# Two of four weight-block sums as transfers that add in SBUF, in a two-layer hybrid attention trunk

## The chip, the cores and the metric

The kernel runs on one core of one Trainium2 chip. The metric is the device time of one execution in microseconds (us); the median of several runs of each kernel counts. All arithmetic is in fp32. TensorE multiplies, VectorE (DVE), ScalarE (ACT) and GpSimd (POOL) do the elementwise work, SyncE (SP) issues most transfers, and each engine works through its own instructions strictly in order. Issuing engines other than SP put their transfers into that same order: a transfer that GpSimd issues waits its turn among GpSimd's instructions.

## The reference

A sequence of 512 tokens with 1024 features passes through two layers. Each has a feed-forward stage, a token mixer (latent attention in layer 0, a compressed, selected and windowed attention in layer 1), and a second feed-forward stage:

```python
def swiglu(x, w_gate, w_up, w_down):
    return (jax.nn.silu(x @ w_gate) * (x @ w_up)) @ w_down

for i in range(DEPTH):                       # DEPTH = 2
    h = h + 0.5 * swiglu(rmsnorm(h, ffn_norm_a[i]), ffn_a_w_gate[i], ffn_a_w_up[i], ffn_a_w_down[i])
    m = rmsnorm(h, mix_norm[i])
    h = h + mixer(m)
    h = h + 0.5 * swiglu(rmsnorm(h, ffn_norm_b[i]), ffn_b_w_gate[i], ffn_b_w_up[i], ffn_b_w_down[i])
return rmsnorm(h, final_norm)
```

Gate and up matrices are 1024 x 2816, the down matrix 2816 x 1024. There are four feed-forward stages; the change touches these alone.

## The kernel before, in words

**Precision.** Every fp32 operand of a product is split in two tiles, high and low: ACT rounds it to the high tile (L170, or L143 for weights of a plain slab), DVE subtracts to get the low tile (L171, L145). A product is three matmuls, high by high, high by low and low by high.

**A feed-forward stage** (`ffn`) runs over 22 blocks of 128 hidden units. Blocks 0 to 2 are multiplied plainly (`plain`). While they run, the inputs are combined for the other blocks (`combine`, tiles `u` and `four`), the row of norms comes out (`row`), and ACT and DVE do the gates (`gate`, tile `tg`: silu at L376) and their products (`act`, tiles `tu`, `ah`, `al`). Blocks 3 to 21, that is 19 in each stage and 76 in all, use a scheme of seven products in place of eight on half blocks: `wsums` prepares the weight blocks and `product` multiplies one of them.

**The weight sums of one block** (`wsums`, L306 to L343). SP loads the gate slab `rg` (L315; the tile is called `rg` in the first block of a stage, `wr` in the others) and the up slab `ru` (L317), each 128 x 1024. Their halves of 512 columns are g0, g1, u0 and u1. In order, the code:

- splits g0 and g1 as loaded (weights 1 and 2),
- puts s1 = u0 + u1 into the tile `s1` (L336, shown as `s` in the profile),
- adds g0 to u0 in place (L337) and splits `ru`, which now holds u0 + g0 and u1 (weights 7 and 4),
- adds s1 to g0 in place (L339), then that sum to g1 in place (L340), and splits both (weights 6 and 3),
- splits s1 (weight 5).

So there are four DVE sums of 128 x 512 a block. Raw `wr` tiles have two buffers; the tag "fr", which `ru`, the first block's `rg` and, in the first stage, the tiles `xt` of the input share, has three; `s1` has one.

**The seven products** go in the order 1, 7, 6, 2, 5, 4, 3. Between them ACT copies partial results out of PSUM (L481, L483, L485, L488: tiles `pg`, `uq`), since the later products add to them. After a block's products come its gate, and two or three `unit`s of the down-projection of blocks that are done: each loads a slab `wdr` of 128 x 384 from SP (L405, two buffers), splits it into `wd` (L170, L171), multiplies it and adds the result to `h` (L399).

**What sets the order.** The code is written in its natural order, and a scheduler places each engine's instructions ahead of time: it may take the split of a later block ahead of the evictions of the present one, and issue a load as early as buffers allow. What it has placed is run in order, each instruction waiting for its semaphores. GpSimd issues nothing in the feed-forward stages of this kernel; at their ends and in the mixers it does sums of squares (L254) and some splits.

Of the kernel before, what the change touches and what calls it, by code (L numbers as in the profile page):

```python
# [11 lines left out]
F32 = mybir.dt.float32  # L12
# [3 lines left out]
ALU = mybir.AluOpType  # L16
AX = mybir.AxisListType

P = 128
S = 512  # L20
# [41 lines left out]
class Kern:  # L62
# [243 lines left out]
    def wsums(self, idx, f):  # L306


        nc, fp, w_gu = self.nc, self.fp, self.a["w_gu"]
        if f == PLAIN:  # L310

            rg = fp.tile([P, 1024], F32, tag="fr", bufs=3, name="rg")
        else:
            rg = self.wp.tile([P, 1024], F32, tag="wr", bufs=2, name="wr")
        nc.sync.dma_start(rg, w_gu[idx, f, 0])  # L315
        ru = fp.tile([P, 1024], F32, tag="fr", bufs=3, name="ru")
        nc.sync.dma_start(ru, w_gu[idx, f, 1])  # L317
        s1 = fp.tile([P, S], F32, tag="s1", bufs=1, name="s1")
        g0, g1, u0, u1 = rg[:, :S], rg[:, S:], ru[:, :S], ru[:, S:]

        def split(src, pool, tag, bufs):
            n = src.shape[1]
            if pool is self.wp:
                hi, lo = self.wtiles("half")
            elif n == 1024:
                hi, lo = self.sum_tiles(n)
            else:
                hi = pool.tile([P, n], F32R, tag=tag[0], bufs=bufs, name="wh")
                lo = pool.tile([P, n + 2 * PAD], F32R, tag=tag[1], bufs=bufs, name="wl")[:, 2 * PAD :]
            self.split(src, hi, lo)  # L330
            return [(hi[:, x : x + S].rearrange("p (k c) -> p k c", c=P), lo[:, x : x + S].rearrange("p (k c) -> p k c", c=P))
                    for x in range(0, n, S)]

        w = {}
        w[1], w[2] = split(rg, self.wp, None, 2)
        nc.vector.tensor_tensor(s1, u0, u1, op=ALU.add)  # L336
        nc.vector.tensor_tensor(u0, u0, g0, op=ALU.add)  # L337
        w[7], w[4] = split(ru, fp, ("fh", "fl"), 3)
        nc.vector.tensor_tensor(g0, g0, s1, op=ALU.add)  # L339
        nc.vector.tensor_tensor(g1, g1, g0, op=ALU.add)  # L340
        w[6], w[3] = split(rg, fp, ("fh", "fl"), 3)
        w[5], = split(s1, fp, ("sh", "sl"), 2)
        return w  # L343
# [994 lines left out]
```

## Time and profile before

| | us |
|---|---|
| three runs | 1894.01, 1894.78, 1894.7 |
| their median | 1894.7 |
| span of the profiled execution | 1891.5 |
| bytes moved in the span | 183.26 MB, 97 GB/s on the mean |

One row of a timeline gives the start in us, the duration, the engine, the line, the operation with the tile that it writes and those that it reads, and in brackets the idle time of the engine just before it and what released it. SPq is SyncE's queue as it issues. A row of waits names the waiting engine and line, and what it waited for. The four feed-forward stages hold nearly all of the time from 0 to 360, 575 to 895, 930 to 1255 and 1565 to 1891.5 us; the mixers lie between.

### The profile page before, as it was taken

What the parts mean: (1) busy time and instruction counts of PE and PEld (TensorE: products, weight loads), DVE (VectorE), ACT (ScalarE), POOL (GpSimd) and SP (SyncE); (2) the same over time, 40 slices, a digit from 0 to 9 for tenths busy, and PEclk for the clock granted to TensorE, in tenths of its full rate; (3) what the DMA queues carried; (4) which work ended last, traced back from release to release, by engine and by line L of the source; (5) the groups of instructions that cost most, each with busy time, mean ns of one, the idle gap of its engine ahead of it and who ended that gap; (6) DMA issues with size and microseconds to landing.
All of it is one profiled execution on the core that took longest, in us unless ns stands there. A gap on an engine that the chain in (4) does not pass through costs nothing.

```text
span 1891.5 us, 33006 instructions
## 1 busy us (share of the span) xinstructions
PE 1865.3 (99%) x12510; PEld 1696.1 (90%) x12510; DVE 1527.3 (81%) x2884; ACT 1091.4 (58%) x2031; POOL 291.8 (15%) x351
## 2 busy tenths in 40 slices
PE   8999999999999999999999999999999999999998
PEld 8999999878879999998999999988788889999997
DVE  8988886677779888886988888666988989888885
ACT  7555554478756555554655555435887866555553
POOL 0000000257720000001100000032666530000000
PEclk9999999999999999999999999999999999999999
DMA  6433331311133333322433332143122133333321
GB/s 231 138 101 100 103 99 41 112 54 46 59 105 117 113 108 105 101 75 60 162 105 101 108 113 87 43 148 106 57 65 70 34 120 117 110 107 107 102 77 67
DMA packets 75903, 183.26 MB, mean 97 GB/s; under 512 B 9041, under 2 KB 37073, under 8 KB 75745
## 3 DMA queue, kind: packets, MB, share of 16 engines
q1 hardware_dynamic: 72800, 176.39, 29.7%
q10 hardware_dynamic: 2944, 4.77, 0.7%
q8 instruction: 98, 1.61, 0.4%
q14 instruction: 61, 0.49, 0.1%
HBM read 178.96 MB, written 2.16 MB: 96 GB/s over the span
## 4 chain that ended last, share of the span: by engine, by line
PE 85%; DVE 7%; ACT 5%; issue 2%; POOL 1%; DMA 1%; SPq 0%; DVEq 0%; ACTq 0%; POOLq 0%
PE pd L163 8%; PE pd L162 8%; PE pd L164 8%; PE px L350 5%; PE px L351 5%; PE px L352 5%; PE pg L350 4%; PE pg L352 4%; PE pg L351 4%; PE pq L352 4%; PE pq L350 4%; PE pq L351 4%; ACT p L643 1%; PE o L1149 1%; PE po L162 1%
## 5 line engine op out<-in xcount | busy, mean ns | idle before, releaser
L163 PE MATMUL pd<-al,wd 128*128 128x512 f32 x576 | 225.0, 391 | 0.0
L162 PE MATMUL pd<-ah,wd 128*128 128x512 f32 x576 | 224.8, 390 | 0.0
L164 PE MATMUL pd<-ah,wd 128*128 128x512 f32 x576 | 224.6, 390 | 0.0
L254 POOL TENSOR_TENSOR s<-s,sq 128x512 f32<-128x512 f32 x38 | 54.8, 1441 | 1062.6 <-ACT sq L250 1059.5
L171 DVE TENSOR_TENSOR w<-wr,w 128x1024 fp32r<-128x1024 f32 x72 | 88.1, 1224 | 135.5 <-ACT w L170 135.5
L350 PE MATMUL px<-four,wh 128*128 128x256 f32 x608 | 168.6, 277 | 0.1
L352 PE MATMUL pq<-four,wl 128*128 128x256 f32 x608 | 167.9, 276 | 0.3 <-DVE wl L171 0.3
L352 PE MATMUL px<-four,wl 128*128 128x256 f32 x608 | 168.0, 276 | 0.0
L350 PE MATMUL pq<-four,wh 128*128 128x256 f32 x608 | 167.9, 276 | 0.0
L351 PE MATMUL px<-four,wh 128*128 128x256 f32 x608 | 167.9, 276 | 0.0
L351 PE MATMUL pq<-four,wh 128*128 128x256 f32 x608 | 167.8, 276 | 0.0
L399 DVE SCALAR_TENSOR_TENSOR h<-pd,h 128x512 f32<-128x512 f32 x216 | 147.5, 683 | 13.9 <-PE pd L164 13.8
L143 ACT ACTIVATE w<-wr 128x1024 fp32r<-128x1024 f32 (+5 forms) x120 | 100.6, 844 | 97.5 <-issue 19.6
L170 ACT ACTIVATE wd<-wdr 128x384 fp32r<-128x384 f32 x192 | 99.2, 519 | 98.5 <-ACT wd L170 63.0
L164 PEld LDWEIGHTS pd<-ah,wd 128*128 128x128 f32 x576 | 108.2, 188 | 22.9
L162 PEld LDWEIGHTS pd<-ah,wd 128*128 128x128 f32 x576 | 108.1, 188 | 20.3
L163 PEld LDWEIGHTS pd<-al,wd 128*128 128x128 f32 x576 | 108.1, 188 | 19.6
L145 DVE TENSOR_TENSOR w<-wr,w 128x1024 fp32r<-128x1024 f32 (+4 forms) x81 | 84.2, 1041 | 49.2 <-ACT w L143 48.5
L643 ACT ACTIVATE p<-p,small 128x512 f32<-128x512 f32 (+2 forms) x192 | 106.5, 556 | 19.8 <-DVE small L642 16.9
L171 DVE TENSOR_TENSOR wd<-wdr,wd 128x384 fp32r<-128x384 f32 x192 | 105.2, 550 | 14.8 <-ACT wd L170 13.9
L350 PEld LDWEIGHTS px<-four,wh 128*128 128x128 f32 x608 | 114.1, 188 | 1.3 <-ACT pg L481 0.8
L170 ACT ACTIVATE w<-wr 128x1024 fp32r<-128x1024 f32 x72 | 76.5, 1062 | 66.4 <-PE pg L352 62.4
(348 smaller groups left out, 6243.9 us busy)
## 6 DMA issues: line engine op xcount, KB each, us to landing
wr<-in_w_gu SPq DMA_DIRECT2D x96, 512.0 KB, 3.3
ru<-in_w_gu SPq DMA_DIRECT2D x76, 512.0 KB, 4.1
wdr<-in_w_down SPq DMA_DIRECT2D x192, 192.0 KB, 2.4
wr<-in_w_down SPq DMA_DIRECT2D x24, 256.0 KB, 2.6
wr<-in_mla_w_o SPq DMA_DIRECT2D x8, 512.0 KB, 3.3
wr<-in_nsa_w_q SPq DMA_DIRECT2D x8, 512.0 KB, 3.3
th<-btab_d SPq DMA_DIRECT2D x16, 256.0 KB, 3.5
wr<-in_nsa_w_o SPq DMA_DIRECT2D x8, 512.0 KB, 3.5
```

What stands on the lines that cost most here:

```text
L143: self.copied = nc.scalar.activation(wh[:, m], raw[:, m], AF.Copy)
L145: nc.vector.tensor_tensor(wl[:, m], raw[:, m], f32v(wh[:, m]), op=ALU.subtract)
L162: mm(out, wh, xh, start=first, stop=False)
L163: mm(out, wh, xl, start=False, stop=False)
L164: return mm(out, wl, xh, start=False, stop=last)
L170: nc.scalar.activation(hi, src, AF.Copy)
L171: (nc.gpsimd if pool else nc.vector).tensor_tensor(lo, src, f32v(hi), op=ALU.subtract)
L350: mm(out, wh[:, p], xh, start=first and p == 0, stop=False, skip_group_check=True)
L351: mm(out, wh[:, p], xl, start=False, stop=False, skip_group_check=True)
L352: mm(out, wl[:, p], xh, start=False, stop=last and p == KP - 1, skip_group_check=True)
L399: nc.vector.scalar_tensor_tensor(self.h[c], p, 0.5, self.h[c], op0=ALU.mult, op1=ALU.add)
L643: nc.scalar.activation(p_sb[:, :n], p_sb[:, :n], AF.Exp, bias=nm, scale=-1.0, accum_out=sm)
```

## The change

Two of the four sums of each block are taken from DVE. SP now also loads u0 into `s1`. GpSimd issues two transfers that read from HBM and add to what lies in SBUF: g0 is added to u0 in `ru` (new L321), and u1 is added to u0 in `s1` (new L322). `s1` gets a second buffer. The sums of L339 and L340 stay on DVE, one line later in the new kernel, as all that follows. The gate and up slabs are still loaded whole, so u0, u1 and g0 are each read from HBM a second time.

```diff
         ru = fp.tile([P, 1024], F32, tag="fr", bufs=3, name="ru")
         nc.sync.dma_start(ru, w_gu[idx, f, 1])
-        s1 = fp.tile([P, S], F32, tag="s1", bufs=1, name="s1")
+        s1 = fp.tile([P, S], F32, tag="s1", bufs=2, name="s1")
+        nc.sync.dma_start(s1, w_gu[idx, f, 1, :, :S])
         g0, g1, u0, u1 = rg[:, :S], rg[:, S:], ru[:, :S], ru[:, S:]
+        nc.gpsimd.dma_start(u0, w_gu[idx, f, 0, :, :S], accum_op=ALU.add)
+        nc.gpsimd.dma_start(s1, w_gu[idx, f, 1, :, S:], accum_op=ALU.add)
...
         w[1], w[2] = split(rg, self.wp, None, 2)
-        nc.vector.tensor_tensor(s1, u0, u1, op=ALU.add)
-        nc.vector.tensor_tensor(u0, u0, g0, op=ALU.add)
         w[7], w[4] = split(ru, fp, ("fh", "fl"), 3)
```

DVE loses 152 instructions, GpSimd gains 152 transfers, SP 76 loads of `s1`. The scheduler places the splits on ACT anew. The start of the first stage on ACT, from the norm row of its first seven-product blocks to their first eviction, before:

```order
L454 ACTIVATE row_405<-pb_400 128x512
L170 ACTIVATE wh_587<-s1_571 128x512
L376 ACT_TABLE_LOAD
L376 ACTIVATE tg_407<-tg_407 128x512
L376 ACTIVATE tg_417<-tg_417 128x512
L170 ACTIVATE four_561<-u_555 128x1024
L170 ACTIVATE ah_413<-tu_411 128x512
L170 ACTIVATE w_572<-rg_567 128x1024
L170 ACTIVATE ah_423<-tu_421 128x512
L376 ACTIVATE tg_544<-tg_544 128x512
```

The split of that block's `ru` stands four rows further, behind three small reads of PSUM (L465). The same place in the changed kernel:

```order
L455 ACTIVATE row_405<-pb_400 128x512
L170 ACTIVATE wh_578<-ru_569 128x1024
L170 ACTIVATE wd_708<-wdr_710 128x384
L170 ACTIVATE wh_768<-s1_751 128x512
L377 ACT_TABLE_LOAD
L377 ACTIVATE tg_407<-tg_407 128x512
L377 ACTIVATE tg_417<-tg_417 128x512
L170 ACTIVATE four_561<-u_555 128x1024
```

The split of `ru_569` has moved from behind the silu to ahead of its table load, 12 rows earlier, with the split of the second block's `s1` and one of `wdr` behind it.

In the second stage, ACT's rows from the first block's first eviction (`pg_6819`) to its last, before:

```order
L481 ACTIVATE pg_6819<-px_6817 128x256
L170 ACTIVATE wh_6992<-s1_6976 128x512
L483 ACTIVATE uq_6820<-pq_6818 128x256
L170 ACTIVATE wh_6982<-ru_6974 128x1024
L485 ACTIVATE uq_6820<-px_6817 128x256
L170 ACTIVATE w_7156<-wr_7151 128x1024
L488 ACTIVATE pg_6819<-px_6817 128x256
```

And in the changed kernel, where the eviction's tile is `pg_6839` and the third block's `s1` is `s1_7176`:

```order
L482 ACTIVATE pg_6839<-px_6837 128x256
L170 ACTIVATE wh_7003<-ru_6994 128x1024
L484 ACTIVATE uq_6840<-pq_6838 128x256
L486 ACTIVATE uq_6840<-px_6837 128x256
L170 ACTIVATE w_7180<-wr_7172 128x1024
L170 ACTIVATE wh_7193<-s1_7176 128x512
L489 ACTIVATE pg_6839<-px_6837 128x256
```

The split of the third block's `s1`, which stood two rows behind the last eviction, now stands ahead of it.

On SP, a steady block of the first stage, before, where `wr` is the slab of the next block but one and `wdr` those of the down-projection:

```order
L315 DMA wr_2127<-in_w_gu 128x1024
L317 DMA ru_2487<-in_w_gu 128x1024
L405 DMA wdr_1945<-in_w_down 128x384
L405 DMA wdr_2090<-in_w_down 128x384
L405 DMA wdr_2107<-in_w_down 128x384
```

And in the changed kernel:

```order
L319 DMA s1_2320<-in_w_gu 128x512
L315 DMA wr_2136<-in_w_gu 128x1024
L317 DMA ru_2498<-in_w_gu 128x1024
L406 DMA wdr_1953<-in_w_down 128x384
L406 DMA wdr_2099<-in_w_down 128x384
L406 DMA wdr_2116<-in_w_down 128x384
```

The load of `s1` stands first, ahead of the slabs. The sums that it feeds are issued by GpSimd; at the start of the second stage they stand behind the last sum of squares of the stage's input, in pairs:

```order
L254 TENSOR_TENSOR s2_6226<-s2_6226,sq_6498 128x512
L321 DMA ru_6814<-in_w_gu 128x512
L322 DMA s1_6816<-in_w_gu 128x512
L321 DMA ru_6994<-in_w_gu 128x512
L322 DMA s1_6996<-in_w_gu 128x512
L321 DMA ru_7174<-in_w_gu 128x512
L322 DMA s1_7176<-in_w_gu 128x512
```

Before, the sum of squares was GpSimd's last instruction until the next mixer's input.

## The prediction

> **What bounds the kernel now.** I read the page first (busy time), then one window for each of the four feed-forward stages, then the waits of TensorE (PE), and last the order of time on ACT and DVE at the places that the change touches.
>
> ```profile
> span 1891.5 us, 33006 instructions
> PE 1865.3 (99%) x12510; PEld 1696.1 (90%) x12510; DVE 1527.3 (81%) x2884; ACT 1091.4 (58%) x2031; POOL 291.8 (15%) x351
> ...
> 40.00:355.00 315.00, 314.72 (x2188) 291.06 (x2187) 258.19 (x392) 161.40 (x263) 9.58 (x7) 1.00 0.32 100
> 580.00:890.00 310.00, 309.18 (x2233) 289.51 (x2232) 253.98 (x396) 158.74 (x259) 1.34 (x1) 1.00 0.31 94
> 935.00:1250.00 315.00, 314.65 (x2192) 291.22 (x2191) 253.94 (x385) 160.52 (x262) 13.72 (x19) 1.00 0.31 96
> 1570.00:1857.00 287.00, 287.00 (x2088) 269.51 (x2088) 238.75 (x365) 148.57 (x243) 0.00 (x0) 1.00 0.32 98
> ```
>
> The window rows give length, then busy time of PE, weight loads, DVE, ACT and POOL, then granted clock, DMA share and GB/s. In the stages that the change touches, PE is idle for 0.28 + 0.82 + 0.35 + 0.00 = 1.5 us of 1227 us, at full clock. DVE is 82% busy there and is not what PE waits for. So work taken from DVE can return 1.5 us in the loops, and otherwise only where a feed-forward stage starts. The median of the runs, 1894.7 us, is 3.2 us above this span; I add those 3.2 us at the end.
>
> **What is removed.** Two DVE sums in each of 76 blocks:
>
> ```profile
> L336 DVE TENSOR_TENSOR s<-ru x76: 674/682/689, 29.6 to 1820.3; 128x512 f32<-128x512 f32 x76
> L337 DVE TENSOR_TENSOR ru<-ru,wr x72: 675/686/694, 50.9 to 1821.0; 128x512 f32<-128x512 f32 x72
> L337 DVE TENSOR_TENSOR ru<-ru,rg x4: 675/679/681, 41.9 to 1559.1; 128x512 f32<-128x512 f32 x4
> ```
>
> That is 152 x 0.68 = 104 us of DVE time, beside PE work almost everywhere. What it can return is bounded by PE's waits for DVE:
>
> ```profile
> PE pg L364 <- DVE w L145: 1.6, 3, 0.8
> PE pg L363 <- DVE x L174: 0.9, 2, 0.7
> PE pb L288 <- DVE small L269: 0.8, 2, 0.6
> PE pu L364 <- DVE w L145: 0.8, 1, 0.8
> ```
>
> The columns are us in total, times, and the longest. Together 4.1 us. Two sums (1.2 us start to start) stand ahead of some of these waits. Bounds 0 and -4.1; I take **-1.0 us**.
>
> **What is added.** For each block one 256 KB load from SP into `s1`, and two 256 KB accumulating transfers from GpSimd: 0.75 MB beside the 1.5 MB that a block loads already (`rg`, `ru`, and `wdr` at 192 KB x 2.7). No row shows an accumulating transfer. The nearest:
>
> ```profile
> wr<-in_w_gu SPq DMA_DIRECT2D x96, 512.0 KB, 3.3
> ru<-in_w_gu SPq DMA_DIRECT2D x76, 512.0 KB, 4.1
> wdr<-in_w_down SPq DMA_DIRECT2D x192, 192.0 KB, 2.4
> wr<-in_w_down SPq DMA_DIRECT2D x24, 256.0 KB, 2.6
> DMA to landing us min/median/max: 3.1/4.1/7.2
> ```
>
> Let D be its time from issue to landing. A plain load of the size takes 2.6 us, the lower end. The longest landing of `ru` (last row) is 7.2 us; twice that, 14.4 us, is the upper end, an estimate for a transfer that must read what it adds to as well. I take D = 2 x 2.6 = 5.2 us (it reads two operands), and 2 x (3.3 - 2.6) = 1.4 us for one more queued ahead of it.
>
> [...]
>
> **Steady blocks: hidden.** Once a stage runs, the buffers lead far enough.
>
> ```profile
> 111.26 0.63 ACT L170 ACTIVATE wh<-s 128x512 fp32r<-128x512 f32 x1 [0.18 <-PE px L351]
> ...
> 132.82 0.33 SPq L317 DMA_DIRECT2D ru<-in_w_gu  x1
> ...
> 172.10 0.64 ACT L170 ACTIVATE wh<-s 128x512 fp32r<-128x512 f32 x1 [0.18 <-PE px L351]
> 173.46 1.06 ACT L170 ACTIVATE wh<-wr 128x1024 fp32r<-128x1024 f32 x1 [0.45 <-PE pq L351]
> 174.87 1.07 ACT L170 ACTIVATE wh<-ru 128x1024 fp32r<-128x1024 f32 x1 [0.35 <-PE pg L351]
> ```
>
> The `ru` issued at 132.82 is split at 174.87, 42 us later. The two `wh<-s` rows lie four blocks apart, 15.2 us a block; with two `s1` buffers a slot is refilled about 30 us before its next use, against 2.6 + 5.2 us needed. In SP's new order the `s1` load stands ahead of `rg`, `ru` and `wdr`, but the slot it waits for is freed before theirs (split of `s` at 172.1, of `wr` at 173.5, of `ru` at 174.9), so they are not held up. Cost 0.
>
> **First stage start.** Here ACT now asks for the accumulated `ru` 12 rows earlier, ahead of the silu:
>
> ```profile
> 23.36 0.33 SPq L317 DMA_DIRECT2D ru<-in_w_gu  x1
> ...
> 32.18 0.62 ACT L170 ACTIVATE wh<-s 128x512 fp32r<-128x512 f32 x1
> 32.81 1.28 ACT L376 ACT_TABLE_LOAD   x1
> ...
> 41.86 0.68 DVE L337 TENSOR_TENSOR ru<-ru,rg 128x512 f32<-128x512 f32 x1
> 43.67 1.23 DVE L171 TENSOR_TENSOR wl<-ru,wh 128x1024 fp32r<-128x1024 f32 x1
> 44.95 0.39 PE L352 MATMUL pq<-four,wl 128*128 128x256 f32 x1 [0.28 <-DVE wl L171]
> ```
>
> `ru` had landed when L336 read it at 29.6 (quoted above). Two `s1` loads ahead of it push that by 2 x 0.7 us to 31.0, and the sum is there at 36.2. ACT wants it at 32.2 and waits 4.0 us. Behind the waiting instruction stand `wd`, the split of the next `s1`, the table load and the silu of two gates; then come 1.06 + 0.52 + 0.62 us less overlap, about 2.0 us, so the table load starts near 38.2 instead of 32.8. DVE waits for the silu, so its `w<-rg` ends 5.4 us later, at 47.3. L337 and the split of `s` no longer stand between it and `wl<-ru`, which ends at 48.4 instead of 44.8. PE already waits for that split (0.28 us at 44.95), so it loses all of it: **+3.6 us** (1.0 at D = 2.6, 12.8 at D = 14.4).
>
> **Third block of the later stages.** Its `s1` reuses the slot of the first block, whose last reader is L339:
>
> ```profile
> 598.22 0.68 DVE L339 TENSOR_TENSOR rg<-rg,s 128x512 f32<-128x512 f32 x1
> 605.58 1.06 ACT L170 ACTIVATE w<-wr 128x1024 fp32r<-128x1024 f32 x1
> 607.44 0.37 ACT L488 ACTIVATE pg<-px 128x256 f32<-128x256 f32 x1 [0.79 <-PE px L352]
> ...
> 936.24 0.68 DVE L339 TENSOR_TENSOR rg<-rg,s 128x512 f32<-128x512 f32 x1
> 944.16 1.06 ACT L170 ACTIVATE w<-wr 128x1024 fp32r<-128x1024 f32 x1 [0.99 <-PE pg L352]
> ...
> 1575.83 0.69 DVE L339 TENSOR_TENSOR rg<-rg,s 128x512 f32<-128x512 f32 x1
> 1583.18 1.05 ACT L170 ACTIVATE w<-wr 128x1024 fp32r<-128x1024 f32 x1
> ```
>
> Slot free at 598.9, load 2.6, sum 5.2: 606.7. The new ACT order splits `s1` right after `w<-wr`, at 606.6, ahead of the eviction of 607.44 that PE's next product needs. So any D over about 5 us delays PE here. The other two stages come out likewise (sum there at 944.7, split wanted at 945.2; 1584.3 and 1584.2). With one transfer queued ahead (D = 6.6) they lose 1.5 + 0.9 + 1.5 = **+3.9 us** (0 at D = 2.6, 27.3 at 14.4). GpSimd itself is free in time: in the second stage its last sum of squares ends at 569.61 + 1.42 = 571.0, and 571.0 + 5.2 = 576.2 against a split wanted at 576.7.
>
> ```profile
> 569.61 1.42 POOL L254 TENSOR_TENSOR s<-s,sq 128x512 f32<-128x512 f32 x1 [0.74 <-ACT sq L250]
> 576.71 1.06 ACT L170 ACTIVATE four<-u 128x1024 fp32r<-128x1024 f32 x1 [0.37 <-DVE u L238]
> ```
>
> **Crowded queues.** From the list of all waits:
>
> ```profile
> ACT wd L170 <- DMA wdr<-in_w_down: 28.5, 42, 2.1
> ```
>
> `wdr` has two buffers and is split soon after landing; ACT already waits for it 42 times, up to 2.1 us, and the evictions behind it then wait too. At a stage's start four or five accumulating transfers catch up beside these loads. I charge one longest wait a stage, 4 x 2.1 = **+8.4 us** (0 if PE's queue covers them). [...]
>
> Sum: 3.6 + 3.9 + 8.4 - 1.0 = +14.9 us; 1891.5 + 14.9 + 3.2 = **1909.6 us**.
>
> **Rivals.** (1) *All hidden*: D near 2.6 and no crowding, 1.0 - 1.0 = 0: 1894.7 us. For it: the long lead of steady blocks; against: the ACT rows of the first start. (2) *Faster*: the transfers land before ACT asks, so the DVE relief counts alone, up to -4.1: 1890.6 us. It decides at D under about 1.2 us at the first start, less than any load row. (3) *Dear sums*: D near 14.4, so 12.8 + 27.3 + 8.4 - 1.0 = +47.5: 1942 us. (4) *Saturation*: if one sum holds all 16 DMA engines longer than 15.2 x 0.63 / 2 = 4.8 us (their share is 0.32 now, and 0.05 more with the `s1` load, a sixth of today's bytes), the steady blocks stall too, 2 x 76 us for each us beyond: over 1960 us. (5) *The change does nothing to DVE*: excluded, its 152 rows are gone from DVE's order.
>
> **How the numbers follow.** Forecast (1898.5 to 1925) 0.47; all hidden 0.22; dear 0.17; saturation 0.07; faster 0.07. A difference of 0.2% (3.8 us) is about what can be told from none: faster 0.07, same 0.22, slower 0.71. The range 1893 to 1945 leaves out the faster case, saturation and the end of the dear one.
>
> **What would show it.** Right: PE's waits list names ACT splits of `ru` or `s1` near 45 us and in the first three blocks of each stage, waits of ACT for GpSimd's transfers or for `wdr`, and none in later blocks; DVE busy falls by 104 us. Wrong: PE idle unchanged (rival 1), or PE waits in every block (rival 4), or a span grown outside these stages.

## The result, and the profile after

| | median us | from, to | ratio to before |
|---|---|---|---|
| before | 1894.36 | 1893.6, 1894.78 (4 runs) | |
| changed | 1918.57 | 1913.38, 1919.15 (4 runs) | 1.0123, 95% interval 1.0111 to 1.0135 |

The change costs 24.2 us between the medians, between 1.2 and 1.3%. The forecast was 1909.6 us, with a range of 1893 to 1945. The profiled execution of the changed kernel is the fastest of its four, 1913.38 us; its span is 20.1 us above that of before, and these 20.1 us are what its trace can explain. First its page:

```profile
span 1911.6 us, 33570 instructions
PE 1872.0 (98%) x12510; PEld 1700.6 (89%) x12510; DVE 1436.1 (75%) x2732; ACT 1083.5 (57%) x2031; POOL 422.8 (22%) x503
```

DVE is busy 91.2 us less than before (1527.3 less 1436.1): 0.60 us for each of the 152 sums. A sum's row is 0.68 us long, but the next instruction starts before it has ended (before, the sum at 29.59 us is followed at 30.19). TensorE got nothing for it. Where the time went is seen with one window for each stage's seven-product loop, from its first product to its last (columns as in the prediction). Before:

```profile
42.30:319.60 277.30, 277.02 (x2012) 259.47 (x2011) 231.87 (x358) 143.28 (x235) 0.00 (x0) 1.00 0.32 100
599.40:875.90 276.50, 276.50 (x2011) 259.59 (x2010) 227.41 (x351) 142.28 (x233) 0.00 (x0) 1.00 0.31 96
938.00:1215.10 277.10, 276.75 (x2011) 259.68 (x2010) 226.81 (x350) 141.78 (x233) 0.00 (x0) 1.00 0.31 96
1577.00:1853.50 276.50, 276.50 (x2011) 259.58 (x2010) 229.60 (x353) 144.65 (x235) 0.00 (x0) 1.00 0.33 101
```

And in the changed kernel:

```profile
45.90:326.60 280.70, 278.09 (x2012) 260.03 (x2010) 209.24 (x321) 139.98 (x233) 29.62 (x34) 1.00 0.57 146
609.00:889.10 280.10, 277.82 (x2012) 260.13 (x2012) 205.29 (x314) 139.44 (x232) 28.68 (x33) 1.00 0.55 142
952.00:1230.10 278.10, 277.04 (x2011) 259.67 (x2010) 205.02 (x313) 139.32 (x232) 28.74 (x33) 1.00 0.55 143
1592.80:1873.90 281.10, 277.44 (x2011) 259.80 (x2010) 209.80 (x320) 142.80 (x235) 28.71 (x33) 1.00 0.56 146
```

Two things are to be seen. The loops are longer by 3.4, 3.6, 1.0 and 4.6 us, 12.6 us in all, and the share of the DMA engines' time has gone from 0.32 to 0.56 for half as many bytes again (146 GB/s against 100). And the loops begin later: the first by 3.6 us (45.9 against 42.3); from the end of one loop to the start of the next 2.6, 0.8 and 0.8 us are added; the tail is 0.3 us shorter. 12.6 + 3.6 + 2.6 + 0.8 + 0.8 - 0.3 = 20.1 us, the whole.

The waits of ACT and of TensorE in the changed kernel (us in total, times, longest):

```profile
ACT wd L170 <- DMA wdr<-in_w_down: 90.8, 43, 4.2
ACT wh L170 <- DMA s<-in_w_gu: 12.5, 7, 4.1
PE pb L288 <- DVE small L269: 5.2, 4, 2.5
PE px L351 <- ACT uq L486: 5.1, 8, 1.6
PE px L351 <- ACT pg L482: 3.5, 2, 2.1
```

Before, ACT waited 28.5 us for `wdr`, and TensorE 0.8 us for the norm (`pb` <- `small`); its list has no row like this table's last two. The transfers, in the changed kernel's table of DMA:

```profile
q1 hardware_dynamic: 83744, 196.32, 32.5%
q0 software_dynamic: 21888, 39.86, 12.7%
wdr<-in_w_down SPq DMA_DIRECT2D x192, 192.0 KB, 3.4
s<-in_w_gu POOLq DMA_DIRECT2D x76, 256.0 KB, 5.9
ru<-in_w_gu POOLq DMA_DIRECT2D x76, 256.0 KB, 4.3
```

The medians from issue to landing of the accumulating transfers are 4.3 and 5.9 us. GpSimd's queue (q0) holds the engines 12.7 / 39.86 = 0.32% of their time per MB, the other queue (q1) 32.5 / 196.32 = 0.17%: here a byte that is added costs about twice a byte that is copied. `wdr` now lands after 3.4 us instead of 2.4.

**Inside a stage.** The second block of the second stage, on ACT, before:

```profile
616.16 0.53 ACT L170 ACTIVATE wd<-wdr 128x384 fp32r<-128x384 f32 x1 [0.51 <-DMA wdr<-in_w_down]
617.15 0.37 ACT L481 ACTIVATE pg<-px 128x256 f32<-128x256 f32 x1 [0.46 <-PE px L352]
```

And in the changed kernel, with what TensorE waited for:

```profile
627.01 0.37 ACT L482 ACTIVATE pg<-px 128x256 f32<-128x256 f32 x1 [1.46 <-PE px L353]
631.56 0.52 ACT L170 ACTIVATE wd<-wdr 128x384 fp32r<-128x384 f32 x1 [4.18 <-DMA wdr<-in_w_down]
631.99 0.36 ACT L484 ACTIVATE uq<-pq 128x256 f32<-128x256 f32 x1
632.25 0.38 ACT L486 ACTIVATE uq<-px 128x256 f32<-128x256 f32 x1
...
632.68 0.39 PE L351 MATMUL px<-four,wh 128*128 128x256 f32 x1 [1.63 <-ACT uq L486]
```

ACT stands at the split of a `wdr` that has not landed, the evictions stand behind it, and the next product needs the PSUM that they empty.

**At a stage's start.** The second stage before: PE takes up the norm without a wait, and ACT splits the second block's `s1` only inside the loop:

```profile
587.50 1.13 PE L288 MATMUL pb<-ident,small 128*128 128x128 f32 x8
...
602.30 0.61 ACT L170 ACTIVATE wh<-s 128x512 fp32r<-128x512 f32 x1
```

And in the changed kernel, ACT, DVE and PE:

```profile
589.52 0.63 ACT L170 ACTIVATE wh<-s 128x512 fp32r<-128x512 f32 x1 [3.12 <-DMA s<-in_w_gu]
590.05 1.04 ACT L170 ACTIVATE four<-u 128x1024 fp32r<-128x1024 f32 x1
591.13 1.23 DVE L171 TENSOR_TENSOR four<-u,four 128x1024 fp32r<-128x1024 f32 x1 [2.05 <-ACT four L170]
...
595.53 1.13 PE L288 MATMUL pb<-ident,small 128*128 128x128 f32 x8 [2.55 <-DVE small L269]
```

The split of the second block's `s1` was placed ahead of the stage's own input work. Its sum landed late, so ACT's split of `four` came late, DVE waited for it with the rest of the norm's short chain (`small`) behind, and TensorE waited 2.55 us for the norm.

**The clock.** Behind that wait, and behind one of 1.79 us in the first stage, the granted clock fell:

```profile
33.70:37.10 3.40, 3.40 (x18) 3.40 (x18) 3.40 (x5) 3.31 (x6) 0.75 (x1) 0.50 1.01 257
596.90:600.30 3.40, 3.40 (x18) 3.40 (x18) 2.32 (x4) 2.82 (x4) 0.00 (x0) 0.50 0.85 324
```

3.4 us at half clock cost 1.7 us each, in which TensorE counts as busy.

### The profile page after: what moved, and what is told of

The parts are those of the page before. It is cut to its first block, busy times and chain, and to the rows that moved or that the text cites. A ratio compares the mean times of both kernels' runs of the same rounds, so it can differ in the third digit from the quotient of the medians.

```text
span 1911.6 us, 33570 instructions
## 1 busy us (share of the span) xinstructions
PE 1872.0 (98%) x12510; PEld 1700.6 (89%) x12510; DVE 1436.1 (75%) x2732; ACT 1083.5 (57%) x2031; POOL 422.8 (22%) x503
## 3 DMA queue, kind: packets, MB, share of 16 engines
q1 hardware_dynamic: 83744, 196.32, 32.5%
q0 software_dynamic: 21888, 39.86, 12.7%
## 4 chain that ended last, share of the span: by engine, by line
PE 72%; DVE 10%; DMA 7%; ACT 6%; issue 3%; POOL 1%; SPq 0%; ACTq 0%; DVEq 0%; POOLq 0%
PE pd L162 7%; PE pd L163 7%; PE pd L164 7%; PE px L351 5%; PE px L353 5%; PE px L352 5%; DMA wdr<-in_w_down 3%; PE pg L353 3%; PE pg L351 3%; PE pg L352 3%; PE pq L351 3%; PE pq L353 3%; PE pq L352 3%; DMA s<-in_w_gu 2%; DVE wl L171 2%
## 5 line engine op out<-in xcount | busy, mean ns | idle before, releaser
L322 POOL DMA_DIRECT2D s<-in_w_gu x76 | 66.7, 878 | 585.6 <-DVE wl L171 472.7
L321 POOL DMA_DIRECT2D ru<-in_w_gu x76 | 66.2, 871 | 341.9 <-DMA ru<-in_w_gu 167.1
L164 PEld LDWEIGHTS pd<-ah,wd 128*128 128x128 f32 x576 | 108.2, 188 | 23.1
```

The source lines that it names most:

```text
L164: return mm(out, wl, xh, start=False, stop=last)
```

## The experiments

All times are medians; each ratio is to runs of the kernel before on the same chip.

### The changed kernel again

> The changed kernel once more, as the base of the other runs. All theories: 1913 to 1919 us, as its first four executions. What its trace can add: the first traced execution lay at the low end (1913.4 us) of executions that else took 1918 to 1919 us. If the difference is TensorE's clock after the two waits at stage starts, a slower traced execution shows more windows under 0.9 granted clock; if it is wdr landing late, ACT's wait for wdr is over the 90.8 us of the first trace.

Measured: 1920.02 us (1913.47 to 1922.04), ratio 1.0127 (1.0107 to 1.0148), 1 us above the expected range; the traced execution had a span of 1919.8 us. Its wait of ACT for `wdr` is 90.5 us, as in the first trace, but the longest is 5.2 us instead of 4.2. It has four steps of the clock within the stages where the first trace has two; the two more are

```profile
634.90:638.30 3.40, 3.20 (x15) 3.20 (x16) 1.42 (x2) 1.54 (x3) 0.00 (x0) 0.50 0.64 126
1624.80:1628.20 3.40, 3.40 (x18) 3.40 (x18) 2.25 (x3) 1.05 (x3) 0.00 (x0) 0.50 0.29 67
```

each at a long wait of ACT for a `wdr` split (4.8 and 5.2 us). So these two executions differ in how long single waits get, and in the clock steps that the longest bring: about 3.4 us of the 8.2 us between the two spans are the two steps. This trace also shows a wait that the prediction described: in the third stage the third block's `s1` lands late, and the split of it stands ahead of an eviction. In the first trace that cost TensorE nothing.

```profile
964.66 0.63 ACT L170 ACTIVATE wh<-s 128x512 fp32r<-128x512 f32 x1 [1.74 <-DMA s<-in_w_gu]
...
965.62 0.38 PE L351 MATMUL pg<-x,wh 128*128 128x256 f32 x1 [1.07 <-ACT pg L489]
```

### Copies in place of accumulating transfers

```diff
-        nc.gpsimd.dma_start(u0, w_gu[idx, f, 0, :, :S], accum_op=ALU.add)
-        nc.gpsimd.dma_start(s1, w_gu[idx, f, 1, :, S:], accum_op=ALU.add)
+        nc.gpsimd.dma_start(u0, w_gu[idx, f, 0, :, :S])
+        nc.gpsimd.dma_start(s1, w_gu[idx, f, 1, :, S:])
```

> The two transfers of a block stay on GpSimd, at the same place in every engine's order, but only copy and add nothing (so the sums u0 + g0 and u0 + u1 are left out of what is computed). Theory A (the adding makes the transfers dear: they hold the 16 DMA engines about twice as long as copies and wdr, whose split stands ahead of evictions, lands late): landing of s falls from 5.9 to under 4.5 us, share of GpSimd's queue from 12.7% to 6-7%, ACT's wait for wdr from 90.8 to under 65 us, time 1900 to 1908. Theory B (the order of ACT, DVE and SP costs, whatever the transfers take): 1912 to 1919. [...]

Measured: 1899.21 us (1898.0 to 1901.28), ratio 1.0024 (1.0015 to 1.0034). From its table of DMA and its waits:

```profile
q0 software_dynamic: 12160, 39.86, 6.1%
wdr<-in_w_down SPq DMA_DIRECT2D x192, 192.0 KB, 2.6
s<-in_w_gu POOLq DMA_DIRECT2D x76, 256.0 KB, 4.5
ru<-in_w_gu POOLq DMA_DIRECT2D x76, 256.0 KB, 3.1
...
ACT wd L170 <- DMA wdr<-in_w_down: 51.2, 44, 2.8
```

The engines' orders are the same (but for one load of tokens that ACT issues a row earlier, near 12 us), the bytes from HBM are the same, GpSimd issues the same instructions. Without the adding, the packets fall from 21888 to 12160 and the share from 12.7% to 6.1%, `wdr` lands after 2.6 us, and 20.8 us of the 26.0 that the changed kernel lost in these runs are gone. Theory A holds; the order (B) and the issue by GpSimd explain at most the rest, 5.2 us.

### The same copies from SP

```diff
-        nc.gpsimd.dma_start(u0, w_gu[idx, f, 0, :, :S])
-        nc.gpsimd.dma_start(s1, w_gu[idx, f, 1, :, S:])
+        nc.sync.dma_start(u0, w_gu[idx, f, 0, :, :S])
+        nc.sync.dma_start(s1, w_gu[idx, f, 1, :, S:])
```

> The same two copies, adding nothing (the two sums are left out), issued by SP behind the loads that they overwrite. Theory A: as with copies from GpSimd within 4 us, 1898 to 1908. Theory B: 1912 to 1919. [...]

Measured: 1901.44 us (1900.5 to 1905.64), ratio 1.0038 (1.0023 to 1.0052). It is not below the copies from GpSimd (1899.21 us), so issue by GpSimd costs no more here than issue by SP.

### No transfers and no sums

```diff
-        nc.gpsimd.dma_start(u0, w_gu[idx, f, 0, :, :S], accum_op=ALU.add)
-        nc.gpsimd.dma_start(s1, w_gu[idx, f, 1, :, S:], accum_op=ALU.add)
```

> The two transfers of a block are taken out, and DVE does not add either (the two sums are left out of what is computed); the load into s1 and its second buffer stay. Theory A: 1890 to 1898, ACT's wait for wdr near the 28.5 us of before. Theory B: over 1905. It also bounds what the two DVE sums were worth: by the prediction at most 4.1 us below 1894.4.

Measured: 1895.97 us (1894.98 to 1896.74), ratio 1.0009 (1.0000 to 1.0018). This is the changed kernel with its two transfers free, and it is still not faster than before. Its loops take 277.1, 276.8, 276.4 and 276.7 us, 0.4 us less in all than before: the relief of DVE is worth no more than that there. ACT's wait for `wdr` is 36.2 us. But the first loop starts at 46.1 us, as late as in the changed kernel. Before, and in this kernel, the last squares of the input on ACT:

```profile
23.57 1.06 ACT L420 ACTIVATE xt<-xt 128x1024 f32<-128x1024 f32 x1 [0.24 <-DMA xt<-in_x_tok]
```

```profile
26.99 1.06 ACT L419 ACTIVATE xt<-xt 128x1024 f32<-128x1024 f32 x1 [2.59 <-DMA xt<-in_x_tok]
```

The fourth load of tokens, from which the first norm is made, lands late. In this study's kernels whose SP issues two loads into `s1` near 12 us, ahead of it, these squares start at 25.4 to 27.4 us (the changed kernel's at 26.84); in those without, at 23.1 to 24.7, but for one told of below. So the late start comes with the plain loads of `s1`, not with the accumulating transfers. How they delay this load is not shown: ACT issues it near 19.3 us before and in the changed kernel alike. Nor does lateness alone make 3.6 us: here and in the changed kernel a clock step follows at 33.7 us; in the kernel with copies from GpSimd the squares are as late (26.68 us), no step follows, and the first loop starts at 44.1 us.

### Three buffers for wdr

```diff
-            raw = ap.tile([P, NG * P], F32, tag="dr", bufs=2, name="wdr")
+            raw = ap.tile([P, NG * P], F32, tag="dr", bufs=3, name="wdr")
```

> The changed kernel with three buffers instead of two for wdr, so that its loads can be issued one unit earlier. Theory D (what the accumulating transfers cost inside the stages is that wdr lands late and ACT, in order, holds the evictions behind its split): ACT's wait for wdr falls from 90.5 to under 40 us, the idle of TensorE at L351 nearly goes and with it the clock steps that follow, 1903 to 1911 us. Theory E (the 16 engines are too busy, whichever load comes late): the wait moves to other loads or splits, 1914 to 1922.

Measured: 1907.75 us (1904.48 to 1908.39), ratio 1.0068 (1.0053 to 1.0083). ACT's wait for `wdr` is 1.3 us in all, and two of the loops are as before:

```profile
610.10:886.80 276.70, 276.70 (x2011) 259.62 (x2010) 203.83 (x314) 141.92 (x232) 28.69 (x33) 1.00 0.55 143
1592.20:1868.90 276.70, 276.70 (x2011) 259.61 (x2010) 206.04 (x316) 144.70 (x234) 28.72 (x33) 1.00 0.55 147
```

at the same DMA share of 0.55. So the engines are not short of time inside a stage; what hurt there was a late `wdr` ahead of evictions on ACT. Theory D holds for the loops. What is left lies at and near the starts: the second and third starts take 2.3 and 2.4 us more (from the end of one loop to the start of the next), the third loop keeps its 1.0 us, and the first loop has 283.2 us, with one wait of 4.0 us and a clock step of 6.83 us. That wait goes back to a split of the accumulated `ru` that stood 2.7 us ahead of the silu, the place that the prediction names.

The scheduler moved something too: 45 splits of `wdr` stand earlier on ACT than in the changed kernel, in the second stage's second block ahead of the first eviction (at 626.5 us) and not behind it. So this run alone doesn't part the buffer from the order. The kernel with copies does: it keeps the changed kernel's order and loses little.

The same buffer in the kernel before:

> The kernel before with three buffers for wdr and nothing else. If the third buffer only undoes what the transfers cause: no change, 1893 to 1896 us. If it is worth something by itself: 1888 to 1891, and part of the 11 us that it brought beside the transfers is not theirs.

Measured: 1894.48 us (1892.73 to 1897.1), ratio 1.0002 (0.9993 to 1.0011). No change: the 11 us that it brought beside the transfers were theirs.

### The first two blocks of each stage on DVE

```diff
+        if f >= PLAIN + 2:
             nc.sync.dma_start(s1, w_gu[idx, f, 1, :, :S])
...
+        if f < PLAIN + 2:
+            nc.vector.tensor_tensor(s1, u0, u1, op=ALU.add)
+            nc.vector.tensor_tensor(u0, u0, g0, op=ALU.add)
```

(and the transfers under the first condition too)

> The first two seven-product blocks of each stage sum on DVE as before, the other 17 by transfers. Theory D says that the stage starts (waits of 2 to 2.8 us for the norm row in two stages, each with a clock step of some 1.7 us) come from splits of sums that have not landed, placed ahead of the norm chain: they go, some 7 to 9 us, and the loops keep theirs: 1908 to 1913 us. If instead any kernel with a crowded start waits there (E): 1915 to 1922.

Measured: 1909.61 us (1909.08 to 1912.82), ratio 1.0085 (1.0070 to 1.0100). The first loop starts at 42.5 us, against 42.3 before; from its end to the second's start are 279.5 us, against 279.8. So the starts are what they were, and the loops keep their loss (283.3, 281.8, 279.7 and 279.5 us). In the first loop the third block's `s1`, the first that a transfer sums here, makes ACT wait 4.9 us.

### Both remedies

> Both remedies at once: the first two seven-product blocks of each stage sum on DVE, and wdr has three buffers; the other 17 blocks of each stage still sum by transfers. If the two mechanisms (late sums at stage starts, late wdr inside the stages) make up the cost: what is left is a little queueing, 1895 to 1901 us, with no wait of 2 us on TensorE and no clock step but at the end. If a third cost of the transfers is hidden below: 1902 to 1908.

Measured: 1907.22 us (1905.02 to 1908.7), ratio 1.0066 (1.0053 to 1.0080). A miss: the remedies don't add. ACT waits 1.7 us for `wdr`, and the second and third loops are 276.8 and 277.3 us; the fourth is 2.4 us longer than before, and why stays open. But the first block that sums by transfers, the third of the first stage, is now the late one. ACT, PE and the window behind:

```profile
67.32 0.63 ACT L170 ACTIVATE wh<-s 128x512 fp32r<-128x512 f32 x1 [8.74 <-DMA s<-in_w_gu]
...
72.03 0.58 PE L356 MATMUL px<-four,wh 128*128 128x256 f32 x1 [6.20 <-ACT pg L487]
...
71.90:78.70 6.80, 6.67 (x35) 6.67 (x36) 5.24 (x10) 1.83 (x4) 0.00 (x0) 0.57 0.69 230
```

One wait of 6.2 us, and a clock step of 6.83 us that starts within it, at 70.90 us (the window shown runs past its end, so its mean is 0.57 and not 0.50). And the first loop starts at 46.3 us again: the fourth load of tokens is late (its squares start at 27.22 us), though no load of `s1` stands near it. `wdr`'s third load stands there, but it does in the kernel before with three buffers too, whose squares start at 23.36; why it is late here stays open. For the late sum no third cost is needed: it has moved to the first block that has one. That is read from two traces, this one and the one above; a kernel in which these first sums start earlier was not tried.

### One of the two transfers

Only u0 + g0 by a transfer, behind DVE's u0 + u1. In the kernel before, with two buffers for `s1`:

```diff
         nc.vector.tensor_tensor(s1, u0, u1, op=ALU.add)
-        nc.vector.tensor_tensor(u0, u0, g0, op=ALU.add)
+        nc.gpsimd.dma_start(u0, w_gu[idx, f, 0, :, :S], accum_op=ALU.add)
```

> Only u0 + g0 is made by a transfer, after DVE has made u0 + u1; no second load of u0. One accumulating transfer a block instead of two, 0.25 MB more a block instead of 0.75. If the cost goes with the time that transfers hold the engines: about a third to a half of +25, so 1901 to 1908. If it sets in only where the queues are full: within 3 us of before, 1892 to 1898.

Measured: 1902.56 us (1901.29 to 1905.41), ratio 1.0047 (1.0032 to 1.0062).

Only u0 + u1 by a load and a transfer, in the changed kernel:

```diff
-        nc.gpsimd.dma_start(u0, w_gu[idx, f, 0, :, :S], accum_op=ALU.add)
+        nc.vector.tensor_tensor(u0, u0, g0, op=ALU.add)
```

> Only u0 + u1 is made by a load and a transfer that adds; u0 + g0 stays on DVE. One accumulating transfer a block, 0.5 MB more a block. If the cost goes with engine time: half to two thirds of +25, so 1905 to 1912, more than with u0 alone. If it sets in only where the queues are full: 1893 to 1900.

Measured: 1909.37 us (1905.81 to 1912.16), ratio 1.0078 (1.0061 to 1.0095). Both sizes were as expected if the cost goes with engine time, but the traces say that this is not how it arises: with u0 alone two of the loops lose nothing (276.4 and 276.8 us), `wdr` lands after 2.4 us as before, and the 8.0 us that this trace has more are 8.1 in the first loop and 1.1 in the third, with 1.2 gained ahead of the second. With s1, `wdr` lands after 3.0 us and ACT waits 91.9 us for it, as much as in the changed kernel. A sum by a transfer costs where something in order stands behind it. The first loop with u0 alone shows it:

```profile
35.84 1.06 ACT L170 ACTIVATE wh<-ru 128x1024 fp32r<-128x1024 f32 x1 [3.08 <-DMA ru<-in_w_gu]
...
44.82 1.21 DVE L171 TENSOR_TENSOR w<-rg,w 128x1024 fp32r<-128x1024 f32 x1
...
46.09 0.58 PE L352 MATMUL px<-x,w 128*128 128x256 f32 x1 [3.24 <-DVE w L171]
```

ACT waits for the accumulated `ru` ahead of the silu, DVE splits `rg` late, and TensorE waits 3.2 us for it. A clock step of 6.83 us starts within that wait. This is the chain that the prediction gave for the first stage.

Then u0 + g0 by transfers in the last 17 blocks of each stage alone:

> One accumulating transfer (u0 + g0) in the last 17 blocks of each stage, both sums of the first two and all sums u0 + u1 on DVE; no second load of u0. With u0 alone the later stages' loops lost nothing, and its cost lay at the starts, which this leaves to DVE: 1893 to 1897 us. If 68 sums taken from DVE were worth something, under 1892; if the late sums only move to the third block, 1899 to 1903.

Measured: 1896.93 us (1894.65 to 1899.65), ratio 1.0013 (1.0004 to 1.0022). 68 sums fewer on DVE and only one wait of TensorE over 1 us in the loops (1.9 us, in the first), and still not faster than before. With the bound that the kernel without transfers gives, no version of this change was found that beats the kernel before.

### The sums on GpSimd itself

```diff
-        nc.vector.tensor_tensor(s1, u0, u1, op=ALU.add)
-        nc.vector.tensor_tensor(u0, u0, g0, op=ALU.add)
+        nc.gpsimd.tensor_tensor(s1, u0, u1, op=ALU.add)
+        nc.gpsimd.tensor_tensor(u0, u0, g0, op=ALU.add)
```

(in the kernel before)

> No transfers: the two sums of each block are made by GpSimd as elementwise sums (L254's take 1.44 us each, so 76 x 2 x 1.44 = 219 us on an engine that is idle in the stages). If what the changed kernel lost is the transfers' and not the handing over of work to GpSimd: 1892 to 1899 us. If a sum that comes later from another engine costs whatever makes it: over 1903.

Measured: 1914.28 us (1911.15 to 1918.08), ratio 1.0105 (1.0092 to 1.0119). A miss in which neither theory comes out clean. DVE's work beside the sums grew. GpSimd's row of one of the sums, and DVE's split of `ru`, which took 1215 ns before:

```profile
L336 POOL TENSOR_TENSOR s<-ru 128x512 f32<-128x512 f32 x76 | 156.0, 2053 | 701.6 <-ACT wh L170 523.1 <-issue 65.1 <-DVE rg L339 56.0
...
L171 DVE TENSOR_TENSOR wl<-ru,wh 128x1024 fp32r<-128x1024 f32 x76 | 123.3, 1622 | 0.2 <-ACT wh L170 0.2
```

It takes 1622 ns here. GpSimd's sums take 2.05 and 1.64 us instead of 0.68. ACT's wait for `wdr` is 69.2 us, though `wdr` lands after 2.4 us as before and no transfer is added: this wait can grow without crowded DMA engines. How much of the 20 us is DVE's slower work, and how much that the sum comes later, these runs don't tell.

## Why the prediction was right, step by step

The direction and the main mechanism were right; that the sizes of the first two terms fit is luck. In the first trace the 20.1 us are 3.6 us at the first start, 4.2 at the three later ones and 12.6 in the loops, less 0.3 at the end. The forecast had 3.6, 3.9 and 8.4 - 1.0. The medians lie 4.1 us further apart than the first trace shows.

- **DVE is not what TensorE waits for** (-1.0 taken, bounds 0 and -4.1): right. Worth 0.4 us at most in the loops of the kernel without transfers. DVE's busy time fell by 91.2 us and not by 104, since the rows of the sums overlap their neighbours.
- **D = 5.2 us**, twice a plain load: the size was right, the reason in part. 4.3 and 5.9 us are the medians, and the engines' time for a transfer doubles. But copies from the same queue take 3.1 and 4.5 us already, so the adding itself makes 1.2 to 1.4 us of D.
- **First start, +3.6 us**: the size was met in the changed kernel by luck. ACT did not wait for the accumulated `ru` in the first trace (it split it at 34.87 with no idle time): the tokens came late, TensorE waited 1.8 us for the norm, and a clock step followed. The predicted chain is real all the same. With u0 alone, where the tokens are on time, ACT waited 3.1 us for `ru`, against 4.0 forecast, and TensorE 3.2, against 3.6; in the changed kernel's second trace it is 1.6 and 1.3 us.
- **Third block, +3.9 us**: right in one stage of three. In the third stage ACT waited for the third block's `s1`, 0.6 us in the first trace and 1.7 in the second, and TensorE lost nothing and 1.1 us, against 0.9 forecast. In the second and fourth stages that split waited only for TensorE (0.35 us at 616.84). The sum that was late there was the second block's, already ahead of the norm, and what it cost stands at the second start: 2.6 us, clock step included.
- **Crowded queues, +8.4 us**: the mechanism was right, ACT's split of a late `wdr` ahead of evictions, but not the working. The loops lost 12.6 us in the first trace. The third `wdr` buffer takes away the 8.2 us of the second and fourth; the 1.0 us of the third stay, and in the first (3.4 us) another wait takes their place, so its share stays open. The forecast charged this at the stages' starts alone, where the longest waits lie but not all (those that end at 693.0 and 1707.7 us are in mid-stage), and the longest wait of before, 2.1 us, is not the longest after (4.2 and 5.2). That GpSimd's transfers leave SP's alone, so that this term is 0 and the sum 1901.2, is out: SP's `wdr` lands 1.0 us later beside them (3.4 against 2.4).
- **Steady blocks cost 0**: half right. The sums are hidden there; the loads beside them are not.
- **Not foreseen**: the clock. Two steps in the first trace (3.4 us), four in the second (6.8 us).
- **The rivals**: all hidden (1894.7) is out; the faster one (1890.6) has no room, since even free transfers give 1896.0; dear sums (D near 14.4) are out at 4.3 and 5.9 us. Saturation is out: 12.7% of 1911.6 us over 152 transfers is 1.6 us of all 16 engines for each, where it asked for over 4.8, and at a share of 0.55 two loops of the kernel with three `wdr` buffers run as before.

## What to carry to other kernels

Where an engine is busy but nobody waits for it, work taken from it returns next to nothing, and the price of moving it is all that is measured: here 0.4 us gained, 24 us lost in all. A transfer that adds counted twice in the queues here (12.7% of the engines' time against 6.1% for copies). Where a stage started, it kept its own reader waiting (3.12 us for `s1` in the second stage); inside the stages it delayed the load with the shortest lead (`wdr`, two buffers, split at once: it landed after 3.4 us instead of 2.4). Look for that load first, and for the in-order engine that holds something else behind it. A remedy for one such place, tried alone, may move the wait to the next: of the 24 us, two remedies brought 11 and 9 by themselves and 11 together.

## What the hardware showed

- In the stages of the changed kernel's first trace the granted clock stepped down to 0.50 for 3.41 us behind two waits of TensorE, of 1.79 us (to 32.40 us) and of 2.55 us (to 595.53). Behind the one of 2.08 us that ends at 1598.03 no step followed, nor behind those of 1.63, 1.45 and 1.22 us. So the length of a wait alone did not decide it here, and what did was not shown. In the first loop of the kernel with both remedies a step of 6.83 us, twice as long, came with a wait of 6.2 us.
- The steps within the stages start 563.20 us apart in the changed kernel's first trace, and 563.20, 37.54 and 989.87 us apart in its second: 165, 11 and 290 times 3.413 us, the length of one step. The cause was not shown.
- An accumulating transfer of 256 KB held the engines twice as long as a copy (12.7% against 6.1% for the same 152) in 1.8 times as many packets.
- With GpSimd's elementwise sums beside it, DVE's split of `ru` took a third longer (1215 to 1622 ns) and that of `wdr` a quarter (550 to 678 ns); with GpSimd's transfers they did not (1216 and 552 ns in the changed kernel).
